# Order of loads, rope table per block, nine matmuls at the start: one change to a fused mLSTM and attention layer

## The chip, the cores and the metric

The kernel runs on one core of a Trainium2 chip. The metric is the device time of one execution in microseconds (us), lower is better. An engine takes its instructions in the order in which the program lists them for that engine: PE (TensorE, matrix products), ACT (ScalarE), DVE (VectorE), POOL (GpSimd), and SP (SyncE), which here issues nearly all the DMA transfers. An instruction that waits holds up everything behind it on its engine.

## The reference, cut to what matters

```python
SEQ, D_MODEL = 2048, 1024                 # one sequence, one layer
a   = rmsnorm(x, g_pre)
mix = concat(mlstm_4_heads(a), mla_8_heads(a)) @ w_out
x   = x + rmsnorm(mix, g_post)
m   = rmsnorm(x, g_pre_mlp)
x   = x + rmsnorm(relu(m @ w_up)**2 @ w_down, g_post_mlp)     # 1024 -> 4096 -> 1024

# mlstm: q, k = silu(conv4(a @ w)); v, output gate, input and forget gates from a;
#        chunk by chunk: num = (q k^T * D) v + w_inter * q C;   C = f' C + (i' k)^T v
# mla:   q from a latent of 256, k and v from a latent of 128, 32 rotated columns (rope),
#        softmax(q k^T / sqrt(96), causal) v
```

All data are float32.

## The kernel before, in words

Every large product is made in three matmul passes on a rounded part and a rest of each operand (`mm3`, L226 to L228): ACT rounds an operand (`wh`, `xh`, `ph`: "h" for high) and DVE or POOL subtracts to get the rest (`wl`, `xl`, `pl`). So each weight tile takes the path DMA load `wr`, ACT cast `wh` (L458), DVE or POOL rest `wl` (L463), then PE.

**Stages.** From 0 to about 540 us the input projection and the mLSTM run in four blocks of 512 tokens. A block works through units of 128 output columns: 13, 14, 15 (latents), 0 (gates), 1 to 4 (convolved q and k), 5 to 8 (mLSTM values, products `mv`), 9 to 12 (output gate), and the products of the latents `kp`, `vp`, `qp` and the rope part 17, 18. The mLSTM has four chunks of 128 tokens per block: chunk (b,c) loads its decay matrix `E` (L1157) and weights `iwbc` (L1165) from DRAM, ACT exponentiates `E` (L1172), PE forms `num` (L1192) and the state update `kv` (L1210), ACT squares `num` into `jk` (L1226), DVE writes `ho`, and a DMA stores it to `hT` (L1257). From about 540 to 980 us come the eight attention heads over four query blocks (scores `m` and `S`, probabilities `ph`/`pl`, output `o`), to about 1180 us the output projection, and then the MLP to the end.

**What sets the order.** `Plan.op` registers each piece of work with an engine, an estimated duration, a key (when it is wanted) and the tile buffers that it takes and frees. `Plan.run` plays the list through once and emits instructions in the order that results; `pin` (L236) fixes that order on PE, ACT, DVE and POOL. SP issues DMAs in the order of emission. A list of predecessors given to `pl.op` for a load moves only its place in that order; what is waited for at run time are the data and the buffers.

**Buffers near the change.** The results of `kp`, `vp`, `qp` and `rp` go through a ring of `SG = 4` staging tiles (`ks`, `vs`, `qs`, `rs`), each freed when its store to DRAM (`qkd`, `vd`, `qrd`) has ended. The attention's probabilities have `HB_`/`LB_` buffers of `ph` and `pl`. The rope table starts in block 0: DVE computes angles (`ang`, `kk`), ACT takes the sine, a store writes `trigd`, and `spread` (L1341) copies it row by row into the DRAM table `trep` for all 2048 positions; block b then loads its slice as `tb`. `rotate` (L869) rotates the one shared key row of a block.

**Hand-over to the attention.** While chunk (3,3) runs, SP also issues the first loads of the attention: `QK` (keys and queries of head 0, one group per block, L1499 and L1501), `maskneg`, and `V0` (L1511). The last values unit's evacuation `vext` (L1110) stands on ACT behind the exponentials of chunk (3,3), and the first score product `m` (L1537) needs the PSUM bank that it empties.

Of the kernel before, what the change touches and what calls it, by code (L numbers as in the profile page):

```python
# [10 lines left out]
F32 = mybir.dt.float32  # L11
# [7 lines left out]
P = 128  # L19
# [14 lines left out]
HB_ = 4  # L34
LB_ = 4
# [17 lines left out]
LEAD = 20.0  # L53
VLEAD = 6.0
# [3 lines left out]
BLOCK = 123.0  # L58
XLEAD = 20.0
WLEAD = 22.0  # L60
SPLIT = 10.0
XS0 = 12.0
XS1 = -60.0
CHUNK = 2.0
# [4 lines left out]
LGAIN = 20.0  # L69
CPOOL = True  # L70
KPOOL = ()
VPOS = (2, 2, 2, 4)
KROT = 50.0
# [10 lines left out]
WSTORE = 10.0  # L84
# [10 lines left out]
EV = 8.0  # L95
LASTLINE = [16, "k0", "k1", 9, "k2", "k3", "v0", 10, "v1", "v2", "v3", 11, 17, "q0", "q1", 12, "q2", "q3", 18, "r0", "r1", 5, 6, 7, 8]
LDK = 20.0
PQ = 0.0
# [24 lines left out]
class Plan:  # L123


    HOP, DMA, RATE, SUM = 190.0, 1900.0, 359.0, 4900.0
    late = 0.0

    def __init__(self):
        self.ops, self.rings, self.frees = [], {}, {}  # L130
        self.group, self.groups = None, {}
# [5 lines left out]
    def op(self, eng, ns, fn, after=(), key=0.0, take=(), free=(), kb=0):  # L137


        i = len(self.ops)  # L140
        self.ops.append((eng, ns, fn, list(after), key, take, kb))
        self.groups.setdefault(self.group, []).append(i)
        for ring, holder in free:
            self.frees.setdefault((ring, holder), []).append(i)
        return i

    def run(self):
# [24 lines left out]
        left, moved = len(ops), 0.0  # L172
        while left:
# [31 lines left out]
            end[i] = at[eng] = s + ops[i][1]  # L205
# [12 lines left out]
def trunk(ctx: ExitStack, tc: tile.TileContext, x, xT, pos, wu, wout, wup, wdn, cols, rows, consts, edge, out, dbg=None):  # L218
# [48 lines left out]
    trep = dram.tile([P, 2, SEQ], F32, tag="trep", name="trep")  # L267
# [70 lines left out]

    def load_cst():
        dma(cst[:, K_ID : K_ID + P], consts[:, K_ID : K_ID + P])  # L340
# [25 lines left out]
    def xsplit(b):  # L366
        def pair(j):
# [24 lines left out]
            for s in [slice(0, 1), slice(1, 2)] if b == 0 else [slice(0, 2)]:  # L392
                a = pl.op("SP", 500, lambda s=s: load(s), [first], key=kA(b, 0.65 * (2 * j + s.start) - 3 - XLEAD), kb=256 * (s.stop - s.start))
                for k in range(2 * j + s.start, 2 * j + s.stop):
                    at = kA(b, 0.65 * k - 3)
                    c = pl.op("Activation", 690, lambda k=k: hi(k), [a, o_col], at, take=(f"xh{k}",))
                    d = pl.op("DVE", 700, lambda k=k: lo(k), [c], at, take=(f"xl{k}",), free=[] if here else [("awr", first)])
# [44 lines left out]
    def wsplit(b, u):  # L442
# [27 lines left out]
        for s in pieces:  # L470
            n = s.stop - s.start
            a = pl.op("SP", 500, lambda s=s: load(s), [a0_], key=kA(b, at - WLEAD + WHALF * len(first)), kb=n / 2)
            c = pl.op("Activation", n * 0.833 + 110, lambda s=s: hi(s), [a], kA(b, at - SPLIT), take=() if first else ("wh",))
            d = pl.op(
                "Pool" if slow else "DVE", 148 + 2.104 * n if slow else n / 0.96 + 69, lambda s=s: lo(s), [c] + ([d] if first else []), kA(b, at - SPLIT), take=() if first else ("wl",),
# [127 lines left out]
    def latents_in(b):  # L603
# [4 lines left out]
        def one(i):  # L608
# [32 lines left out]
            if b == 0:  # L641
                o = pl.op("Activation", 560, evac, [u["op"], *t.get("o", [])], key, take=take, free=[("mm", u["head"])])
                head = o
                o = pl.op("DVE", 660, norm, [o, o_rsbc[b]], key, free=[("rsbc", o_rsbc[b])])
# [40 lines left out]
        def split(i):  # L685
# [8 lines left out]
            g = pl.op("DVE", 710, lambda: gain(i), [l, o], late, free=[("cbc", l)])  # L694
# [10 lines left out]
    def operands(b, t, o_c, held):  # L705
# [116 lines left out]
        o_tb = pl.op("SP", 500, table, [o_rope[2 * (b % 2) + 1], t["gained"]], kA(b, TIME[b][18] - 10), take=("cbc",), kb=512)  # L822
# [46 lines left out]
    def rotate(b, t, G):  # L869
# [26 lines left out]
        g = pl.op("SP", 500, load, [o_rope[2 * (b % 2)], G], key, take=("cth",), kb=128)  # L896
# [149 lines left out]
    def conv(b, j):  # L1046
# [39 lines left out]
        for i in range(1, 4):  # L1086
            o = pl.op("DVE", 720, lambda i=i: tap(i), [o], key, free=[("raw", r)])
# [3 lines left out]
            pl.op("DVE", 670, lambda i=i: put(i), [h, *war, *(o_fill3 if j < 2 else [])], key, free=[("cy", y), ("cth", h)])  # L1091
# [35 lines left out]
    def gates(b, h):  # L1127
# [11 lines left out]
        o_gate[b, h] = pl.op("DVE", 440, gain, [o], key)  # L1139

    def chunk(b, c):
# [119 lines left out]
        e = pl.op("SP", 500, load_e, [o_sc_in[b, "wd"]], key, take=("E",), kb=256)  # L1261
        i = pl.op("SP", 1000, load_w, [o_sc_in[b, "wd"]], key, take=("iwbc",), kb=128)
# [25 lines left out]
    def rope_tables():  # L1288
# [7 lines left out]
        def half(q):  # L1296
# [39 lines left out]
            def spread():  # L1336
                for hb in range(2):
                    cs = slice(hb * 1024 + q * 512, hb * 1024 + q * 512 + 512)
                    for x, r0, g0, n in ((0, 0, 0, 8), (1, 48, 0, 4), (1, 32, 4, 4)):
                        to = trep.rearrange("(g j) x t -> g j x t", j=16)[g0 : g0 + n, :, x, cs]  # L1340
                        dma(to, trigd[r0 : r0 + 16, cs].rearrange("(o j) t -> o j t", o=1).broadcast_to((n, 16, 512)))  # L1341

            r = pl.op("SP", 1000, load, [o_x[RB[q], RK[q]][1]], key, take=("raw",), kb=256)
            y = o = pl.op("DVE", 420, d0, [r], key, take=("cy",), free=[("raw", r)])
            o = pl.op("DVE", 480, d1, [o], key)
            h = o = pl.op("DVE", 480, d2, [o], key, take=("cth",))
            o = pl.op("DVE", 500, d3, [o], key)
            for c in (PI2_A, PI2_B, PI2_C):
                o = pl.op("DVE", 690, lambda c=c: d4(c), [o], key)
            o = pl.op("DVE", 480, d5, [o, o2], key)  # L1350
            o = pl.op("DVE", 430, d6, [o], key)
# [3 lines left out]
            o_rope.extend((o, pl.op("SP", 3000, spread, [o], key, kb=1024)))  # L1355
# [139 lines left out]
    def load_qk(h, b, key):  # L1495
# [8 lines left out]
        o = pl.op("SP", 1500, load, [*o_kd[h // 2, b], *o_qd[h // 2, b], o_qr[h // 4, b], o_s3 if s else o_s1, *war], key, kb=640)  # L1504
        o_q[h, b] = [o]
        o_k[h, b] = [o, o_kr[s, b]]

    def load_v(g, t, key):
# [4 lines left out]
        o_v[g, t] = [pl.op("SP", 1000, load, [o_vd[t], o_vd[t + 1], *([o_s3, o_const["v"]] if g else [o_s2, o_const["v0"]])], key, kb=512)]  # L1513
# [314 lines left out]
    def matrix(k):  # L1828
# [16 lines left out]
        a = pl.op("SP", 500, load, [o_s3 if early else o_left], key, take=("wr",), kb=512)  # L1845
        for c in range(2):
            b = pl.op("Activation", 610, lambda c=c: hi(c), [a], key, take=(ring[c],))
            o_w[k, c] = pl.op("DVE", 690, lambda c=c: lo(c), [b], key, free=[("wr", a)])
# [4 lines left out]
    def group(g):  # L1853
# [8 lines left out]
        def tile_(k):  # L1862
# [26 lines left out]
            if heads:  # L1889
                b = pl.op("SP", 1000, loadr, [o_left] + [o_out[h, blk][1] for h in heads], key, take=("rb",), kb=128)  # L1890
                r = pl.op("DVE", 335, norm, [a, b], key, free=[("rb", b)])
            c = pl.op("Activation", 307, hi, [r], key, take=(f"h{k}",))
            return c, pl.op("DVE", 335, lo, [c], key, free=[("hr", a)])
# [21 lines left out]
        def post(t):  # L1915
# [41 lines left out]
            f = pl.op("Pool" if slow else "DVE", 2300 if slow else 1140, add, [d, e], key, free=[("xt", d)])  # L1957
# [748 lines left out]
```

## Time and profile before

| | us |
|---|---|
| time, median of 3 runs | 2447.58 (2446.93 to 2453.14) |
| profiled execution, own time | 2449.75 |
| profiled execution, span in the trace | 2447.8 |
| PE busy in the span | 2384.2 (97%) |
| DVE busy | 1766.5 (72%) |
| ACT busy | 1360.5 (56%) |
| POOL busy | 835.1 (34%) |

Mean granted clock of PE: 0.993 of full speed. The views read below are the page with its chain of waits, the list of what PE waited for, tables of busy time by stretch of the span, and timelines. "Busy" counts an instruction from its modelled start to its modelled end. A row of the timeline gives start, duration, engine, line, operation, tiles, and in brackets the idle time before it with what ended it.

### The profile page before, as it was taken

The numbers are of one execution on the slowest core, as the hardware profiler recorded it, in microseconds if no ns is written. First come the engines' busy times: TensorE is split into PE (matmuls) and PEld (weight loads), VectorE is DVE, ScalarE is ACT, GpSimd is POOL, SyncE is SP. The second block draws the span as 40 slices with busy tenths as digits, with TensorE's granted clock in tenths as the row PEclk, the third lists the DMA queues.
The fourth block names the chain that finished last, engine by engine and source line by source line (L and its number), as shares of the span: only waits on it lengthen the run. The fifth ranks groups of instructions, "written<-read, shape, count | busy, mean of one in ns | idle before, by whom it ended". The sixth has DMA issues, their size and how long they took to land.

```text
span 2447.8 us, 34049 instructions
## 1 busy us (share of the span) xinstructions
PE 2384.2 (97%) x10915; PEld 1918.2 (78%) x10915; DVE 1766.5 (72%) x3153; ACT 1360.5 (56%) x2645; POOL 835.1 (34%) x713
## 2 busy tenths in 40 slices
PE   8899999999999999999999999999999999999998
PEld 6777787777777777788887888888888888888886
DVE  6766666648888888744866677766666687687889
ACT  5545444436777777644665666756665344343455
POOL 3433434436888788632100000000000232322346
PEclk9999999998999999999999999999999999999999
DMA  6696969797322220466777788756664534535348
GB/s 241 223 314 214 327 231 325 251 257 179 93 58 67 56 53 12 111 211 217 264 209 207 227 281 246 220 171 180 198 195 140 182 126 148 159 125 183 126 132 183
DMA packets 341819, 449.20 MB, mean 184 GB/s; under 512 B 34908, under 2 KB 227432, under 8 KB 341640
## 3 DMA queue, kind: packets, MB, share of 16 engines
q1 hardware_dynamic: 337704, 440.16, 58.2%
q0 software_dynamic: 3936, 6.87, 2.0%
q8 instruction: 86, 1.41, 0.2%
q14 instruction: 93, 0.76, 0.1%
HBM read 295.97 MB, written 153.05 MB: 183 GB/s over the span
## 4 chain that ended last, share of the span: by engine, by line
PE 78%; DVE 7%; DMA 6%; issue 3%; ACT 3%; POOL 2%; SPq 1%; DVEq 0%; ACTq 0%; POOLq 0%
PE mm L226 3%; PE mm L227 3%; PE mm L228 3%; PE S L226 3%; PE o L1622 2%; PE S L227 2%; PE S L228 2%; PE o L1625 2%; PE m L1537 2%; PE mv L227 1%; PE mv L228 1%; PE mv L226 1%; PE op L226 1%; PE op L228 1%; PE op L227 1%
## 5 line engine op out<-in xcount | busy, mean ns | idle before, releaser
L2516 POOL TENSOR_TENSOR y<-vd_0X,y 128x512 f32<-128x512 f32 x7 | 11.3, 1620 | 727.7 <-ACT vd_0X L2513 709.8
L1636 POOL TENSOR_TENSOR t<-t,ph 128x512 f32<-128x512 f32 (+1 forms) x192 | 214.4, 1116 | 17.8 <-ACT ph L1601 7.8
L1601 ACT ACTIVATE ph<-S 128x512 fp32r<-128x512 f32 (+1 forms) x320 | 170.2, 532 | 87.2 <-PE S L228 33.4
L2428 ACT CAST hh<-hr 128x512 fp32r<-128x512 f32 (+1 forms) x208 | 116.2, 567 | 150.5 <-DMA hr<-hd 23.8
L1609 DVE TENSOR_TENSOR pl<-S,ph 128x512 fp32r<-128x512 f32 (+3 forms) x272 | 156.7, 590 | 30.3 <-ACT S L1605 27.7
L226 PE MATMUL mm<-xh,wh 128*128 128x512 f32 x384 | 160.3, 417 | 17.1 <-ACT wh L458 8.4
L227 PE MATMUL mm<-xl,wh 128*128 128x512 f32 x384 | 151.7, 395 | 1.5 <-DVE xl L388 1.5
L228 PE MATMUL mm<-xh,wl 128*128 128x512 f32 x384 | 151.6, 395 | 0.7 <-DVE wl L463 0.7
L2433 DVE TENSOR_TENSOR hl<-hr,hh 128x512 fp32r<-128x512 f32 (+1 forms) x208 | 130.2, 637 | 28.2 <-ACT hh L2428 21.6
L1542 DVE TENSOR_REDUCE mp<-m 128x1 f32<-128x512 f32 x192 | 128.6, 681 | 27.1 <-PE m L1537 27.0
L1605 ACT ACTIVATE S<-S 128x512 f32<-128x512 f32 (+3 forms) x272 | 141.0, 519 | 0.3
L226 PE MATMUL S<-QK 97*128 97x512 f32 (+1 forms) x320 | 122.9, 384 | 6.2 <-DVE pl L1609 4.1
L1622 PE MATMUL o<-ph,V 128*128 128x512 f32 (+1 forms) x320 | 121.0, 378 | 0.2 <-DVE ot L1695 0.2
L1537 PE MATMUL m<-QK 96*128 96x512 f32 (+3 forms) x320 | 113.3, 399 | 6.8 <-ACT vext L1110 2.7
L227 PE MATMUL S<-QK 97*128 97x512 f32 (+1 forms) x320 | 118.3, 370 | 0.0
L228 PE MATMUL S<-QK 97*128 97x512 f32 (+1 forms) x320 | 117.9, 368 | 0.0
L1625 PE MATMUL o<-pl,V 128*65 128x512 f32 (+1 forms) x320 | 114.8, 361 | 0.2
L226 PEld LDWEIGHTS mm<-xh,wh 128*128 128x128 f32 x384 | 73.1, 190 | 38.3 <-ACT wh L458 8.4
L226 PE MATMUL op<-wo,hh 128*128 128x512 f32 x256 | 101.2, 395 | 0.7 <-DVE x L1937 0.7
L2267 ACT ACTIVATE t<-t 128x512 f32<-128x512 f32 x96 | 60.6, 631 | 73.8 <-DVE t L2262 73.2
L228 PE MATMUL op<-wo,hl 128*128 128x512 f32 x256 | 99.9, 390 | 0.0
L227 PE MATMUL op<-wo,hh 128*128 128x512 f32 x256 | 99.8, 390 | 0.0
(6442 smaller groups left out, 7581.2 us busy)
## 6 DMA issues: line engine op xcount, KB each, us to landing
hr<-hd SPq DMA_DIRECT2D x100, 448.0 KB
wr<-in_wu_dram SPq DMA_DIRECT2D x71, 512.0 KB
hd<-t SPq DMA_DIRECT2D x128, 256.0 KB
hd<-ts SPq DMA_DIRECT2D x96, 256.0 KB
wl<-wparts SPq DMA_DIRECT2D x45, 512.0 KB
QK<-qkd SPq DMA_DIRECT2D x32, 512.0 KB
xt<-in_x_dram SPq DMA_DIRECT2D x28, 512.0 KB
xf<-xd SPq DMA_DIRECT2D x40, 256.0 KB
```

Of the source, the lines that this page charges most:

```text
L226: pe.matmul(o, ah, bh, start=start, stop=False)
L227: pe.matmul(o, ah, bl, start=False, stop=False)
L228: pe.matmul(o, al, bh, start=False, stop=stop)
L1537: pe.matmul(ps[:, :n], Qh[s][0:96, q0 : q0 + P], Kh[s][0:96, kb * TB : kb * TB + n], start=True, stop=True)
L1542: vec.tensor_reduce(mp["t"][:, j, kb : kb + 1], ps, axis=AX.X, op=ALU.max)
L1601: act.activation(t["h"][:, :w], t["S"][:, :w], AF.Exp)
L1605: act.activation(t["p"][:, :w], t["S"][:, :w], AF.Exp)
L1609: (pool if by_pool else vec).tensor_tensor(t["l"][:, :w], t["p"][:, :w], f32(t["h"][:, :w]), ALU.subtract)
L1622: pe.matmul(o0, v[:, 0:128], t["h"][:, :w], start=start, stop=stop)
L1625: pe.matmul(o1, v[:, 64:129], t["l"][:, :w], start=start, stop=stop)
L1636: pool.tensor_tensor(to, to, hv, ALU.add)
L2433: vec.tensor_tensor(t["l", m][:, :w], t["r", m][:, :w], f32(t["h", m][:, :w]), ALU.subtract)
```

## The change

Constants first, since many edits are numbers of the planner:

```diff
-HB_ = 4 ; LB_ = 4 ; LEAD = 20.0 ; VLEAD = 6.0 ; BLOCK = 123.0
+HB_ = 5 ; LB_ = 5 ; LEAD = 25.0 ; VLEAD = 3.0 ; BLOCK = 119.0
+SPLIT0 = 30.0          # key lead of the weight splits in block 0 (SPLIT = 10 before)
+WARM = 9
-CHUNK = 2.0 ; LGAIN = 20.0 ; KPOOL = ()   ; KROT = 50.0 ; WSTORE = 10.0 ; EV = 8.0  ; PQ = 0.0
+CHUNK = 0.0 ; LGAIN = 40.0 ; KPOOL = (0,) ; KROT = 90.0 ; WSTORE = 5.0  ; EV = 15.0 ; PQ = 5.0
```

`LGAIN` is how late the latents' gain (`cca`, `ccb`) may come; `KPOOL = (0,)` puts the key rotation of block 0 (four operations of 32 x 512) on POOL instead of DVE. The planner also learns that a DVE operation with two inputs from SBUF ("DVES") takes longer while a long POOL operation runs; this changes order only. The other edits:

```diff
+    def warm():
+        act.copy(mrow[0:1, 16:17], zeros[0:1, 0:1])
+    def warm_pe():
+        ps = ps1.tile([P, 4, P], F32, tag="S", name="warm", bufs=2)
+        for i in range(WARM):
+            pe.matmul(ps[:, i % 4], ones, ones, start=True, stop=True)
...
-    trep = dram.tile([P, 2, SEQ], F32, tag="trep", name="trep")
+    trep = [dram.tile([P, 2, TB], F32, tag=f"trep{b}", name=f"trep{b}") for b in range(NB)]
...
-            dma(tb["t"], trep[:, :, bs])
+            dma(tb["t"], trep[b])
+        def spread():
+            for x, r0, g0, n in ((0, 0, 0, 8), (1, 48, 0, 4), (1, 32, 4, 4)):
+                to = trep[b].rearrange("(g j) x t -> g j x t", j=16)[g0 : g0 + n, :, x]
+                dma(to, trigd[r0 : r0 + 16, bs].rearrange("(o j) t -> o j t", o=1).broadcast_to((n, 16, TB)))
+        o = pl.op("SP", 1800, spread, [o_rope[b % 2], t["gained"]], kA(b, TIME[b][18] - 25), kb=512)
...
-            o_rope.extend((o, pl.op("SP", 3000, spread, [o], key, kb=1024)))
+            o_rope.append(o)
...
+    o_last = [o_chunk[NB - 1, 3]["e"], o_chunk[NB - 1, 3]["i"]]     # loads of E and iwbc of chunk (3,3)
-        o = pl.op("SP", 1500, load, [..., *war], key, kb=640)                                      # load_qk
+        o = pl.op("SP", 1500, load, [..., *war, *(o_last if b and not h else [])], key, kb=640)
...
+        if g: after = [o_s3, o_const["v"], o_sc[start_of[2, qb]]]                                  # load_v
+        else: after = [o_s2, o_const["v0"], *([o_sc[start_of[0, qb - 2]]] if qb > 1 else o_last if qb else [])]
...
-        a = pl.op("SP", 500, load, [o_s3 if early else o_left], key, take=("wr",), kb=512)         # output weights
+        a = pl.op("SP", 500, load, [o_sc[start_of[4, 0]] if early else o_left], key, take=("wr",), kb=512)
```

How this moves instructions, in the rows of the program order; a row has the source line, the operation, output and inputs (tile name, block and unit or chunk, buffer number) and the shape. The changed program's line numbers are some 32 to 40 higher.

On DVE, before, in block 0 behind the convolution of `raw0_1`: `ccb`/`cca` are the latents' gains, `qbd`/`cy`/`kT` the convolution, `wl0_5` to `wl0_8` the rests of the four values units.

```order
L681 SCALAR_TENSOR_TENSOR ccb0_325<-ccb0_325,col_61,cbc0_639 128x512
L1057 TENSOR_TENSOR raw0_2_688<-mm0_3_617,rsbc0_444 128x512
L681 SCALAR_TENSOR_TENSOR cca0_324<-cca0_324,col_61,cbc0_639 128x512 x2
L1078 SCALAR_TENSOR_TENSOR qbd0_111<-cth0_1_690,cy0_1_633 64x512 x2
L463 TENSOR_TENSOR wl0_5_733<-wr0_5_423,wh0_5_549 128x1024
L1069 SCALAR_TENSOR_TENSOR cy0_2_705<-raw0_2_688,col_61,cy0_2_705 128x512 x3
L463 TENSOR_TENSOR wl0_6_755<-wr0_6_451,wh0_6_621 128x1024
L1080 SCALAR_TENSOR_TENSOR kT0_113<-cth0_2_757,cy0_2_705 128x512
L463 TENSOR_TENSOR wl0_7_770<-wr0_7_452,wh0_7_673 128x1024
L463 TENSOR_TENSOR wl0_8_777<-wr0_8_501,wh0_8_735 128x1024
```

The same place of the changed program begins with the last of the four rests:

```order
L495 TENSOR_TENSOR wl0_8_748<-wr0_8_503,wh0_8_727 128x1024
L1109 SCALAR_TENSOR_TENSOR cy0_1_626<-raw0_1_245,col_61,cy0_1_626 128x512 x2
L1109 SCALAR_TENSOR_TENSOR cy0_2_742<-raw0_2_707,col_61,cy0_2_742 128x512
L1097 TENSOR_TENSOR raw0_3_772<-mm0_4_659,rsbc0_472 128x512
L1118 SCALAR_TENSOR_TENSOR qbd0_114<-cth0_1_774,cy0_1_626 64x512 x2
L1109 SCALAR_TENSOR_TENSOR cy0_2_742<-raw0_2_707,col_61,cy0_2_742 128x512 x2
L1109 SCALAR_TENSOR_TENSOR cy0_3_797<-raw0_3_772,col_61,cy0_3_797 128x512 x2
L1120 SCALAR_TENSOR_TENSOR kT0_116<-cth0_2_813,cy0_2_742 128x512
L1109 SCALAR_TENSOR_TENSOR cy0_3_797<-raw0_3_772,col_61,cy0_3_797 128x512
L714 SCALAR_TENSOR_TENSOR ccb0_337<-ccb0_337,col_61,cbc0_618 128x512
L714 SCALAR_TENSOR_TENSOR cca0_336<-cca0_336,col_61,cbc0_618 128x512 x2
```

`wl0_5` stands earlier still, ahead of the gate chain `sm0`; the gains have gone from ahead of the rests to behind the convolution. On PE, `num0_0` moved back by 27 matmuls, from among the first products of `mv0_2` to among the first of `mv0_3`.

On SP, before, in the second half of block 0 (`ks` are the staged keys, `xr1` the input of block 1):

```order
L763 DMA qkd_65<-ks0_0_1079 64x2x512 x2
L763 DMA qkd_65<-ks1_0_1083 64x2x512 x2
L453 DMA wr0_12_1161<-in_wu_dram 128x1024
L453 DMA wr0_18_1178<-in_wu_dram 128x512
L1341 DMA trep_69<-trigd_70 128x1x512
L1341 DMA trep_69<-trigd_70 64x1x512 x2
L1341 DMA trep_69<-trigd_70 128x1x512
L1341 DMA trep_69<-trigd_70 64x1x512 x2
L763 DMA qkd_65<-ks2_0_1176 64x2x512 x2
```

In the changed program, from the load of block 0's table to the same store:

```order
L853 DMA tb0_1125<-trep0_69 128x1024
L1374 DMA trigd_73<-kk1_972 64x512 x2
L570 DMA ddx1_1160<-rrx1_1153 4x128
L412 DMA xr1_0_1181<-in_xT_dram 128x2x512
L943 DMA krd_67<-tg0_1053 32x512
L796 DMA qkd_65<-ks2_0_1132 64x2x512 x2
```

Six table copies stood right ahead of the store of `ks2_0`. Now only three are issued in block 0 (`trep0`), ahead of the stores of `ks0_0` and `ks1_0` and of the last weight loads, and none stands between those and the store of `ks2_0`. The other nine follow in blocks 1 to 3, three each.

On SP at the hand-over, before:

```order
L1157 DMA E3_2_4810<-wd3_4289 128x512
L1499 DMA QK0_4769<-qkd_65 64x4x512
L1165 DMA iwbc3_2_4814<-wd3_4289 64x2x128 x2
L1501 DMA QK0_4769<-qrd_66 16x2x512 x2
L1499 DMA QK0_4769<-qkd_65 64x4x512
L1501 DMA QK0_4769<-qrd_66 16x2x512 x2
L1499 DMA QK0_4769<-qkd_65 64x4x512
L1501 DMA QK0_4769<-qrd_66 16x2x512 x2
L1499 DMA QK0_4769<-qkd_65 64x4x512
L1501 DMA QK0_4769<-qrd_66 16x2x512 x2
L1257 DMA hT_64<-ho3_0_4875 128x4x128
L1157 DMA E3_3_4896<-wd3_4289 128x512
```

And after the change:

```order
L1197 DMA E3_2_4828<-wd3_4296 128x512
L1471 DMA maskneg_4788<-in_consts_dram 128x512
L1526 DMA QK0_4787<-krd_67 32x2x512 x4
L1532 DMA QK0_4787<-qkd_65 64x4x512
L1205 DMA iwbc3_2_4834<-wd3_4296 64x2x128 x2
L1534 DMA QK0_4787<-qrd_66 16x2x512 x2
L1297 DMA hT_64<-ho3_0_4880 128x4x128
L1197 DMA E3_3_4887<-wd3_4296 128x512
L1205 DMA iwbc3_3_4910<-wd3_4296 64x2x128 x2
L1532 DMA QK0_4787<-qkd_65 64x4x512
L1534 DMA QK0_4787<-qrd_66 16x2x512 x2
```

The `QK` groups of blocks 1 to 3 and the `V0` loads went from ahead of `E3_3` to behind `E3_3` and `iwbc3_3`; `maskneg` and the rotated keys (`krd`), which stood ahead of `E3_2`, now stand behind it.

More of the change, by code (lines that the diff above doesn't have):

```diff
@@ L33 @@
 WHALF = 0.0
-HB_ = 4
-LB_ = 4
+HB_ = 5
+LB_ = 5
 TAIL = 2
@@ L52 @@
 TLATE = 0.0
[L53 to L54 removed]
+LEAD = 25.0
+VLEAD = 3.0
 SLEAD = 3.0
@@ L894, in lo @@
             eng.tensor_tensor(t["Gr"][s], t["G"][s], t["tg"][s], ALU.subtract)
-        g = pl.op("SP", 500, load, [o_rope[2 * (b % 2)], G], key, take=("cth",), kb=128)
+        g = pl.op("SP", 500, load, [o_rope[b % 2], G], key, take=("cth",), kb=128)
         o = pl.op(*cost, d1, [g, G], key)
@@ L1090, in conv @@
         o_qk[b, j] = [
-            pl.op("DVE", 670, lambda i=i: put(i), [h, *war, *(o_fill3 if j < 2 else [])], key, free=[("cy", y), ("cth", h)])
+            pl.op("DVES", 670, lambda i=i: put(i), [h, *war, *(o_fill3 if j < 2 else [])], key, free=[("cy", y), ("cth", h)])
             for i in range(2 if j < 2 else 1)
```

145 lines of the change are left out of this document (82 added, 63 removed).

## The prediction

> **What bounds the kernel now.** I read the page first, then PE by stretches, then the list of what PE waited for.
>
> ```profile
> PE 2384.2 (97%) x10915; PEld 1918.2 (78%) x10915; DVE 1766.5 (72%) x3153; ACT 1360.5 (56%) x2645; POOL 835.1 (34%) x713
> PE 78%; DVE 7%; DMA 6%; issue 3%; ACT 3%; POOL 2%; SPq 1%; DVEq 0%; ACTq 0%; POOLq 0%
> ```
>
> PE is busy for all but 2447.8 - 2384.2 = 63.6 us, and the matmuls stay the same, apart from nine added ones. So the change can win only PE's idle time and the time that PE runs at a lower clock. The next table has the stretch in us, its length, busy time of PE, PEld, DVE, ACT, POOL (instructions in brackets), granted clock, DMA share, GB/s.
>
> ```profile
> 0.00:123.00 123.00, 106.21 (x474) 84.33 (x474) 85.51 (x173) 66.26 (x124) 50.15 (x51) 0.97 0.69 232
> 123.00:246.00 123.00, 114.85 (x528) 92.29 (x529) 79.45 (x155) 57.50 (x110) 46.25 (x41) 0.99 0.78 263
> 246.00:369.00 123.00, 120.94 (x567) 96.96 (x566) 79.32 (x169) 61.21 (x124) 46.08 (x43) 1.00 0.80 280
> 369.00:492.00 123.00, 116.83 (x529) 90.84 (x528) 79.54 (x158) 55.80 (x104) 53.71 (x46) 1.00 0.85 288
> 492.00:615.00 123.00, 116.25 (x538) 90.57 (x537) 80.40 (x197) 60.72 (x144) 63.51 (x64) 0.92 0.83 215
> 2300.00:2448.00 148.00, 137.23 (x599) 111.55 (x597) 130.37 (x187) 76.82 (x178) 74.98 (x70) 0.98 0.65 155
> ```
>
> Idle per stretch: 16.8, 8.2, 2.1, 6.2, 6.8, and 10.8 in the tail. That is 40 us to 615 us and only 13 us in the 1,685 us after it up to the tail. The clock is below 1 at the beginning and around the hand-over. What PE waited for (total, times, longest):
>
> ```profile
> PE mm L226 <- ACT wh L458: 8.4, 1, 8.4
> PE mv L227 <- DVE wl L463: 4.9, 2, 3.3
> PE mm L226 <- ACT vs L784: 4.3, 1, 4.3
> PE S L226 <- DVE pl L1609: 4.1, 9, 1.3
> PE m L1537 <- ACT vext L1110: 2.7, 1, 2.7
> ```
>
> The waits on `wl`, `vs` and `vext` are three places, and each is followed by a stretch at half the clock:
>
> ```profile
> 8.30:12.70 4.40, 4.33 (x10) 3.42 (x11) 4.28 (x7) 4.35 (x8) 0.00 (x0) 1.00 1.05 393
> 59.70:63.90 4.20, 0.92 (x5) 0.76 (x5) 4.17 (x3) 1.84 (x5) 3.76 (x3) 1.00 0.03 12
> 64.00:70.70 6.70, 5.12 (x12) 3.50 (x12) 6.59 (x9) 1.80 (x5) 2.79 (x3) 0.50 0.89 265
> 124.20:128.60 4.40, 0.08 (x2) 0.07 (x1) 2.08 (x3) 1.17 (x3) 0.41 (x2) 1.00 0.91 334
> 128.80:132.20 3.40, 3.40 (x9) 2.61 (x9) 2.94 (x4) 2.86 (x5) 1.64 (x2) 0.50 0.73 166
> 538.60:541.70 3.10, 0.39 (x3) 0.30 (x2) 0.91 (x2) 2.62 (x12) 2.21 (x4) 1.00 0.92 270
> 541.90:548.60 6.70, 6.03 (x21) 5.25 (x21) 4.64 (x16) 0.00 (x0) 0.93 (x1) 0.50 1.17 294
> 548.70:555.40 6.70, 4.99 (x21) 2.43 (x19) 6.38 (x23) 2.55 (x11) 1.01 (x1) 1.00 0.78 207
> 555.50:569.10 13.60, 13.14 (x39) 9.59 (x40) 8.27 (x20) 4.54 (x11) 3.10 (x7) 0.50 0.94 221
> ```
>
> Nine matmuls take 3.40 us at clock 0.50. At half clock the busy time counts double, so half of it is lost. The first stretch (8.30) shows 1.00 but only 10 matmuls in 4.40 us, which is the same slow pace. These places are where the change acts.
>
> **The change part by part.** All sums are made against the profiled execution's own 2449.75 us, which is 2.2 above the median of the runs shown (2447.58).
>
> *Start.*
>
> ```profile
> 0.94 0.17 DVE L331 MEMSET ones<- 128x128 f32 x1
> 2.19 5.49 DMA wr<-in_wu_dram
> 7.70 1.24 ACT L458 CAST wh<-wr 128x512 fp32r<-128x512 f32 x2 [0.59 <-DMA wr<-in_wu_dram]
> 29.76 0.89 PE rp L590 x8
> ```
>
> The first real matmul waits for the cast of a weight tile that lands at 7.7 us. Loading ACT's table earlier moves the `xh` casts but not this one, so its gain is 0. The four 128 x 128 products of `rp` (eight rows) took 0.89 us, 0.22 each, or 0.44 at half clock. Nine of them on `ones`, ready at 1.1 us, run until about 1.2 + 4.0 = 5.2 us, beside the load. Then PE is idle for some 3.1 us until 8.37. Warmth that lasts would save half of the slow stretch, (12.7 - 8.37)/2 = 2.2 us. In this trace idle times of 2.7 us (before 541.4) and 3.3 us (before 63.0) were each followed by half clock. I take 0, with bounds 0 and -2.2.
>
> [...]
>
> *Block 0, the rests of the values weights (59.7 to 70.7).*
>
> ```profile
> 48.35 1.37 DVE L1078 SCALAR_TENSOR_TENSOR qbd<-cth,cy 64x512 f32<-64x512 f32 x2
> 57.27 3.48 DVE L1078 SCALAR_TENSOR_TENSOR qbd<-cth,cy 64x512 f32<-64x512 f32 x2
> 60.78 2.18 DVE L463 TENSOR_TENSOR wl<-wr,wh 128x1024 fp32r<-128x1024 f32 x1
> 65.49 1.22 DVE L463 TENSOR_TENSOR wl<-wr,wh 128x1024 fp32r<-128x1024 f32 x1
> ```
>
> DVE reaches `wl0_5` only at 60.8, behind the gains and `qbd`, and both are stretched: 3.48 against 1.37 us and 2.18 against 1.22 us, while POOL is busy 3.76 of 4.20 us (the row of 59.70). PE loses 3.3 + 1.6 = 4.9 us waiting, and 5.12/2 = 2.6 us by the clock, together 7.5. In the changed order all four rests stand ahead of most of the convolution, and the gains behind it. That removes both waits. What is late next is the gate chain `sm0`, behind which `wl0_5` no longer waits, and with it `E0_0`. `num0_0` stands 27 matmuls later on PE (27 x 0.24 = 6.5 us, by the step of one matmul in the chain, quoted in the next part), about as much as the four rests put ahead cost at 1.22 to 2.18 us each (4.9 to 8.7). So up to 2.5 us of new wait is possible. I take -6, with bounds 0 and -7.5.
>
> *Block 0, the staging ring (100 to 132).*
>
> ```profile
> 112.45 4.51 SPq L1341 DMA_DIRECT2D trep<-trigd  x6
> 117.26 1.27 SPq L763 DMA_DIRECT2D qkd<-ks  x2
> 117.92 9.13 DMA qkd<-ks
> 127.17 0.70 DVE vs L787
> 106.51 0.24 PE mm L226
> PE mm L226 <- ACT ks L733: 1.8, 2, 1.3
> ```
>
> Six table copies (0.75 us of SP each, 1 MB together) stand right ahead of the store of `ks2_0`. That store takes 9.13 us, and the staging tile that `vs` needs is free only then. PE stood 4.3 us, and 1.8 in smaller waits at the same ring just ahead (the last row, of the waits from 90 to 140 us); the clock costs 3.40/2 = 1.7 more. Total 7.8. Now only three copies are issued in block 0, ahead of the stores, and none between. SP is free 4.5 us sooner for `ks2_0`, and the transfer has less beside it, but the weights and inputs of block 1 stay (DMA share 0.91). The wait of 4.3 needs 4.3 us: 4.5 at SP alone cover it, if the smaller waits stay. I take -6, which is the 4.3 and the 1.7 behind it, with bounds 0 and -7.8.
>
> *Tables of later blocks.* Blocks 1 to 3 get three copies each: 2.25 us of SP and 0.5 MB, some 1.9 us of transfer at 263 to 288 GB/s. Block loads are wanted well ahead, so they hide behind queued tiles; without this cover each block would pay up to 2.25. I take +1 in all (0 to +2, one block in the open).
>
> *Hand-over (538 to 569).*
>
> ```profile
> 523.60 0.69 DVE L1253 TENSOR_TENSOR ho<-ht,gate 128x512 f32<-128x512 f32 x1 [0.59 <-PE ht L1249]
> 530.47 0.53 SPq L1257 DMA_DIRECT2D hT<-ho  x1
> 531.09 0.45 SPq L1157 DMA_DIRECT2D E<-wd  x1
> 538.00 1.28 ACT L1172 ACTIVATE E<-E,tm 128x128 f32<-128x128 f32 x4 [9.44 <-DMA E<-wd]
> ```
>
> `ho` of chunk (3,0) was done at 524.3, but its store went out only at 530.5, behind the `QK` groups on SP, and `E3_3` behind it. ACT waited 9.44 us for that `E`, with `jk` and `vext` queued behind. So `m` started 2.7 us late, with 0.7 more idle in the next stretch (6.70 - 6.03) and 6.03/2 = 3.0 by the clock: 6.5 together. Now `hT` and `E3_3` stand ahead of the later `QK` groups. `E3_3` can go out near 525 instead of 531.1; six us are more than the 2.7 that PE waited, and the wait goes. What is late next: the `QK` and `V0` loads of later blocks, behind it; block 0's `QK`, which the first scores read, stays ahead. The second slow stretch (13.14/2 = 6.6) follows 6.7 us in which DVE was busy 6.38 with the first maxima and PE 4.99. The changed order doesn't remove that work. I take half, -3.3. Sum -9.8, bounds 0 and -13.1.
>
> *Edits with no price of their own.* The key rotation on POOL: four operations of 32 x 512, with POOL idle 72.9 of the first 123 us and the result first read by `QK` at the hand-over; 0, and its cost without cover is bounded by the stretch in the rows of 57 to 61 us, some 3 us on DVE. Later V and output weight loads fall where PE is the bound and are read much later: 0; if one were late, 0.5 MB at 215 GB/s is 2.4 us. A fifth `ph`/`pl` buffer: at most the 4.1 us of waits for `pl`; I take -1. The tail: DVE is busy 130.37 of 148 us there and the same operations stay, so 0 (-3 to +4, from the 10.8 us idle and as a third of it either way). The changed keys shift the other waits of blocks 1 to 3, 8.2 + 2.1 + 6.2 - 4.3 = 12.2 us idle; I take -1.5 (-5 to +5).
>
> **Sum:** 0 - 6 - 6 + 1 - 9.8 - 1 - 1.5 = -23.3, or 2449.75 - 23.3 = 2426.4 against the profiled execution and 2447.58 - 23.3 = 2424.3 against the median. I predict **2425**.
>
> **The rivals.**
>
> *The waits move and do not go.* `num0_0` waits for `E0_0` in place of `mv` for `wl`, the staging ring waits for the same store behind the loads of block 1, or `m` waits for DVE. For it: DVE is 70% busy in block 0 and the DMA queues 0.91 at the staging wait, neither of which gets less. Against it: each wait has a named instruction ahead that moves. It gives a net gain of about 3: 2445.
>
> *All clear.* The full bounds at the three places, -7.5 - 7.8 - 13.1, the warm start's -2.2 and -4 around them give -34.6: 2413. For it: the slow clock comes as a consequence of waits; against it: DVE's reductions after the hand-over.
>
> *The warm clock holds at the start.* Inside my forecast: 2449.75 - 25.5 = 2424.2, against the median 2422. One in four, since 2.7 us of idle were enough for half clock here.
>
> *Slower: DVE becomes the bound of block 0.* The rests, convolution and gains between 40 and 123 us all have to pass DVE beside POOL. If DVE's operations were stretched there throughout by the 3.48/1.37 or 2.18/1.22 of the rows, 85.51 x 83/123 = 58 us of DVE work would become more than the 83 us available; the point from which it decides is 83/58 = 1.4. At 1.7 it is 98 us, 15 too many, in place of the 12 gained there, with the half clock after it (2 or 3): +17, and with the other terms as taken (1 - 9.8 - 1 - 1.5 = -11.3) +6, with the hand-over's gain at nothing +15: 2453 to 2463. Against it: POOL is busy only 50.15 of 123 us, and only one more small job goes there.
>
> *It does not do what it says.* The waits for the DMA data remain whatever the order: that is the first rival's price.
>
> **How the numbers follow.** Forecast, 2416 to 2440: 0.66. All clear, below 2416: 0.11. Waits move, 2440 to 2453: 0.16. Slower: 0.07. The range goes to 2410, below the sum of all bounds, and to 2446, just over the first rival's time; it leaves some 0.05 below and 0.15 above (half of that rival, and all of the slower one). What a measurement of this kernel can tell from no change is about 0.3%, 7.3 us: faster than 2440.3 is 0.66 + 0.11 = 0.77, within is 0.16, slower is 0.07.
>
> **What would show it.** In the changed profile: no wait of `mv` for `wl` of over 1 us and clock 1.00 around 60 to 70 us; no wait for `vs` or `ks` of over 2 us around 100 to 130 us; `E` of chunk (3,3) issued before 527 us, and no wait for `vext`; the second slow stretch in the first scores halved. PE's idle time up to 615 us should fall from 40 to about 25. Wrong would be: a new wait of `num` for `E` near 80 us, the ring waiting again behind block 1's loads, new idle in blocks 1 to 3, or clock 0.50 after the hand-over as before.

## The result, and the profile after

| | before | after |
|---|---|---|
| median, us (5 runs each, beside each other) | 2449.17 (2446.93 to 2453.14) | 2428.12 (2425.68 to 2430.62) |
| profiled execution, own time | 2449.75 | 2430.62 |
| span in the trace | 2447.8 | 2428.9 |

The ratio is 0.9913 with a 95% interval of 0.9899 to 0.9926: 21 us faster, where 2425 was predicted. The profiled execution is the slowest of the five, and it is the one whose trace is read here. First its page, then busy time by the same stretches as before (the last one ends with the span):

```profile
PE 2376.6 (98%) x10933; PEld 1920.0 (79%) x10933; DVE 1748.1 (72%) x3149; ACT 1362.3 (56%) x2646; POOL 832.7 (34%) x717
```

```profile
0.00:123.00 123.00, 112.81 (x509) 90.33 (x510) 94.04 (x174) 72.21 (x133) 59.13 (x59) 1.00 0.72 242
123.00:246.00 123.00, 120.28 (x567) 97.03 (x566) 82.05 (x171) 57.20 (x118) 52.32 (x46) 1.00 0.78 267
492.00:615.00 123.00, 118.88 (x589) 93.83 (x588) 90.42 (x226) 68.02 (x164) 71.69 (x73) 0.94 0.84 193
2300.00:2428.00 128.00, 111.92 (x479) 91.26 (x477) 100.11 (x153) 65.98 (x159) 64.65 (x64) 0.94 0.68 150
```

In the first 123 us PE starts 509 matmuls where it started 474, and the idle time fell from 16.8 to 10.2 us. Part of this is the nine added matmuls, which the trace shows as 18 instructions; they are all that PE does in the first 7.3 us:

```profile
0.00:7.30 7.30, 4.21 (x18) 3.91 (x18) 1.87 (x8) 3.03 (x5) 1.18 (x9) 1.00 0.66 182
```

So 491 of the 509 are the kernel's own, and 4.2 of the 6.6 us of idle time that went are filled with work that nobody needs. Around the hand-over the clock is still at 0.94 in the mean, and in the tail it fell from 0.98 to 0.94 with 16 us idle out of 128: the tail has become worse. The list of waits has no `wl` of 3 us, no `vs` of 1 us (the longest is 0.8) and no `vext` any more; at its head stands a wait of the tail:

```profile
PE d_7X L2519 <- DVE y L2542: 3.0, 1, 3.0
...
PE mm L245 <- DVE ks L769: 2.1, 2, 1.8
...
PE mt L1609 <- DVE mp L1583: 1.9, 1, 1.9
```

Where the time went is read best from groups of matmuls by tile: each row ends with the starts of its first and last instruction. Of before, and then of after:

```profile
L226 PE MATMUL qp<-ch,wh x32: 394/397/400, 135.7 to 500.3; 128*128 128x512 f32 x32
L1622 PE MATMUL o<-ph,V x320: 220/393/628, 564.9 to 1026.2; 128*128 128x512 f32 x144, 128*128 128x256 f32 x16
L2478 PE MATMUL d_0X<-d,hh x64: 388/389/392, 1818.1 to 2373.9; 128*128 128x512 f32 x64
L2480 PE MATMUL d_7X<-d,hl x64: 387/390/498, 1888.6 to 2438.0; 128*128 128x512 f32 x64
```

```profile
L245 PE MATMUL qp<-ch,wh x32: 392/397/422, 125.4 to 487.1; 128*128 128x512 f32 x32
L1663 PE MATMUL o<-ph,V x320: 221/393/628, 545.4 to 1001.3; 128*128 128x512 f32 x144, 128*128 128x256 f32 x16
L2519 PE MATMUL d_0X<-d,hh x64: 389/389/392, 1791.5 to 2346.4; 128*128 128x512 f32 x64
L2521 PE MATMUL d_7X<-d,hl x64: 388/389/628, 1862.3 to 2414.6; 128*128 128x512 f32 x64
```

The differences between these rows give the account of the 18.9 us of span, stage by stage:

| stretch, by its last mark | mark before, after | won so far | won in the stretch | predicted for it |
|---|---|---|---|---|
| input projection and mLSTM (last `qp`) | 500.3, 487.1 | 13.2 | 13.2 | 12.5 |
| hand-over (first `o`) | 564.9, 545.4 | 19.5 | 6.3 | 9.8 |
| attention (last `o`) | 1026.2, 1001.3 | 24.9 | 5.4 | 1 |
| output projection, up (first `d_0X`) | 1818.1, 1791.5 | 26.6 | 1.7 | 0 |
| down and tail (end of the span) | 2447.8, 2428.9 | 18.9 | -7.7 | 0 |

The sum came out near because errors of opposite signs offset each other: the attention won 4.4 us more than predicted, while the hand-over won 3.5 less and the tail gave back 7.7. The 1.7 us of the output projection and the up projection are smaller than their scatter: this stretch takes 790.2 us here, and 788.5, 787.7 and 788.3 us in three of the kernels below whose edits lie outside it (no matmuls at the start, the old tail, the first filling). The experiments ask for the causes.

### The profile page after: what moved, and what is told of

Its sections match the earlier page's. It is cut to its first block, busy times and chain, and to the rows that moved or that the text cites. A ratio compares the mean times of both kernels' runs of the same rounds, so it can differ in the third digit from the quotient of the medians.

```text
span 2428.9 us, 33978 instructions
## 1 busy us (share of the span) xinstructions
PE 2376.6 (98%) x10933; PEld 1920.0 (79%) x10933; DVE 1748.1 (72%) x3149; ACT 1362.3 (56%) x2646; POOL 832.7 (34%) x717
## 4 chain that ended last, share of the span: by engine, by line
PE 53%; DVE 1%; DMA 1%; ACT 0%; issue 0%; DVEq 0%; SPq 0%; POOL 0%; ACTq 0%; POOLq 0%
PE op L245 1%; PE op L247 1%; PE op L246 1%; DMA hr<-hd 1%; PE d_1X L2519 1%; PE d_1X L2520 1%; PE d_3X L2520 1%; PE d_3X L2519 1%; PE d_2X L2519 1%; PE d_2X L2520 1%; PE d_1X L2521 1%; PE d_2X L2521 1%; PE d_7X L2519 1%; PE d_3X L2521 1%; PE d_6X L2519 1%; PE d_0X L2520 1%
```

## The experiments

Each kernel is the changed one with one edit, unless said otherwise. Times are medians; the ratio to before, measured beside it on the same chip, is the safer number across the groups of runs, since before itself read 2446 to 2449 in them. The changed kernel's ratio is 0.9913.

**The order of loads at the hand-over undone.**

```diff
-        o = pl.op("SP", 1500, load, [..., *war, *(o_last if b and not h else [])], key, kb=640)
+        o = pl.op("SP", 1500, load, [..., *war], key, kb=640)
-            after = [o_s2, o_const["v0"], *([o_sc[start_of[0, qb - 2]]] if qb > 1 else o_last if qb else [])]
+            after = [o_s2, o_const["v0"], *([o_sc[start_of[0, qb - 2]]] if qb > 1 else [])]
```

> The changed kernel with one part undone: the QK loads of blocks 1 to 3 and the V0 loads again go out ahead of E and iwbc of chunk (3,3) (only SP's order differs). Theory: the 7 us that the changed kernel gained between the last values products and the first attention output come back, E of chunk (3,3) is issued about 6 us later than in the changed kernel, ACT waits for it with vext or jk behind, and the time is 2432 to 2436. Rival: the gain there came from the order of DVE and ACT at the hand-over, not from the load; then the time is within 2 us of the changed kernel's 2428.

Measured: 2431.35 us, ratio 0.9930 (0.9918 to 0.9942). The timelines of ACT, SP and PE around the load of `E` for chunk (3,3), of the changed kernel and then of this one:

```profile
511.88 0.33 SPq L1197 DMA_DIRECT2D E<-wd  x1
516.76 1.28 ACT L1212 ACTIVATE E<-E,tm 128x128 f32<-128x128 f32 x4 [0.55 <-DMA E<-wd]
```

```profile
515.50 0.45 SPq L1197 DMA_DIRECT2D E<-wd  x1
522.52 1.28 ACT L1212 ACTIVATE E<-E,tm 128x128 f32<-128x128 f32 x4 [7.66 <-DMA E<-wd]
525.16 0.68 ACT L1150 ACTIVATE vext<-mv,rsx 128x512 f32<-128x512 f32 x1
525.89 0.56 PE L1578 MATMUL m<-QK 96*128 96x256 f32 x2 [0.93 <-ACT vext L1150]
```

`E` is issued 3.6 us later, ACT waits 7.66 instead of 0.55 us with `vext` behind, and PE waits for it again. From the last `qp` to the first `o` this kernel takes 62.4 us (485.7 to 548.1), the changed one 58.3. So the mechanism is as predicted, and the order of loads alone is worth 3 to 4 us: 3.2 by the medians and 4.2 by the ratios, whose intervals overlap, 4.1 by the stretch itself. A time of 2432 to 2436 was expected. What won the rest of the 6.3 us there was not tried.

**The rests of block 0 late again.**

```diff
-SPLIT0 = 30.0 ; LGAIN = 40.0
+SPLIT0 = 10.0 ; LGAIN = 20.0
```

> The changed kernel with the old lead of the weight splits in block 0 and the old lead of the latents' gains (SPLIT0 = 10, LGAIN = 20). Theory: wl0_5 comes late on DVE again, PE waits 3 to 5 us for it near 60 us and the clock drops to 0.50 behind it, +5 to +7.5 us: 2433 to 2436. Rival: the planner's stretched DVE durations alone keep the rests early, and the time stays within 2 us of 2428.

Measured: 2431.92 us, ratio 0.9935 (0.9921 to 0.9948). In the list of waits from 40 to 123 us:

```profile
PE mv L246 <- DVE wl L495: 4.7, 1, 4.7
```

The wait for `wl` is back, and the first `qp` starts at 131.0 instead of 125.4 us. At the last `o` the whole 5.8 us are still there (1007.1 against 1001.3), at the first `d_0X` 3.2 (1794.7 against 1791.5). Whether the rest was made up is not shown: the stretch between these marks takes 787.6 us here, no less than in the three kernels named under the table. The edit costs 3.8 us by the medians, a little under what was expected, and 5.4 by the ratios.

**The table in two halves again.** The edit restores `trep` as one DRAM tile, six copies per half.

> The changed kernel with one part undone: the rope table again is one DRAM tensor of all positions, copied in two halves of six DMAs in block 0. Theory: the second half of the copies stands ahead of the stores of the staged keys again, PE waits for the staging ring near 100 to 130 us, +3 to +8 us: 2431 to 2436. Rival: the earlier order of block 0 alone already keeps the stores clear of the copies; then 2426 to 2430.

Measured: 2433.52 us, ratio 0.9941 (0.9928 to 0.9953). The time came back, but not where it was expected. The waits from 90 to 145 us:

```profile
PE qp L245 <- DVE gate L1170: 2.6, 1, 2.6
PE mm L245 <- DVE ks L769: 1.7, 1, 1.7
PE ptx L562 <- POOL rsx L558: 1.6, 1, 1.6
PE vp L245 <- ACT ks L766: 1.0, 1, 1.0
PE vp L245 <- DVE vs L820: 0.7, 1, 0.7
```

PE does not stand 4 us for the staging ring. Its waits there (`ks`, `vs`) come to 3.4 us, where the changed kernel has 2.1 in the same window; the longest wait is for the output gate, and one is for the row statistics `rsx`, both on other engines. The edit also moved instructions on DVE in these blocks, so that this run does not separate the copies' bandwidth from the order that follows from them. At the last `qp` 3.4 us are lost (490.5 against 487.1). A single wait of 4.8 us of `o` near 575 us adds to the profiled execution, which is the slowest of the six.

**Four buffers for the probabilities again.**

```diff
-HB_ = 5 ; LB_ = 5
+HB_ = 4 ; LB_ = 4
```

> The changed kernel with four instead of five buffers for ph and pl. Theory: between the first attention output and the output projection PE loses the 3 to 4 us that the changed kernel gained there (many small waits of S for pl and of o for ph), 2431 to 2433. Rival: that gain comes from other parts of the order, and the time stays within 1.5 us of 2428.

Measured: 2435.25 us, ratio 0.9951 (0.9938 to 0.9964). It has the highest median of the parts undone by themselves, about 7 us above the changed kernel (9 by the ratios), where 3 to 5 were expected. The loss lies in the attention: from the first to the last `o` this kernel takes 464.2 us (543.9 to 1008.1), the changed one 455.9. The waits from 555 to 1000 us, of the changed kernel and then of this one:

```profile
PE o L1663 <- DVE ot L1736: 2.1, 5, 0.7
PE S L245 <- DVE pl L1650: 1.9, 4, 0.8
```

```profile
PE o L1666 <- POOL pl L1650: 2.0, 2, 1.7
PE S L245 <- DVE pl L1650: 1.5, 3, 0.9
PE S L245 <- ACT p L1646: 1.5, 2, 0.8
PE m L1578 <- DVE mp L1583: 1.3, 4, 0.3
```

The waits of `S` for `pl` are about the same; grown or new are waits for `p`, for the row maxima `mp` and for POOL's `pl`. This fits a fifth buffer that lets ACT, DVE and POOL all run ahead, and not only the one wait that names `pl`. But these waits do not explain the size: PE's idle time between the two marks grew by 2.8 of the 8.3 us. Why PE also counts as busy for 5.5 us longer, with 2308 matmuls against 2301 and the clock at 1.00 in both, stays open.

**No matmuls at the start, and nearly twice as many.**

```diff
-WARM = 9
+WARM = 0     # and, in the other kernel, WARM = 17
```

> The changed kernel without the nine matmuls on ones; ACT's early copy stays. Theory: the nine matmuls gave nothing, since the clock was at half again until about 12 to 14 us with them: 2426 to 2430, the same as the changed kernel. Rival: they gave up to 2 us: 2430 to 2432.

> The changed kernel with 17 matmuls on the tile of ones instead of 9, so that PE has work from 1.2 us to about the first weight tile at 7.9 us. [...] Rival: the clock at the start depends on something other than PE's gap (time since the start, or the size of the matmuls); then the real matmuls stay at half clock until about 13 us and the time is 2428 or up to 1 us more.

Measured: 2427.93 us without (0.9918, 0.9904 to 0.9931), 2424.53 with 17 (0.9905, 0.9891 to 0.9918). Busy time from 7.8 to 13.6 us, of the changed kernel and of the one with 17 on ones, and from that kernel's waits up to 60 us the longest behind the start:

```profile
7.80:13.60 5.80, 5.75 (x14) 4.44 (x15) 5.09 (x8) 4.77 (x8) 0.00 (x0) 1.00 1.03 376
```

```profile
7.80:13.60 5.80, 5.44 (x24) 3.56 (x23) 4.87 (x8) 4.60 (x7) 0.00 (x0) 1.00 1.03 373
```

```profile
PE rp L623 <- POOL rsx L558: 1.4, 1, 1.4
```

Nine matmuls change nothing in the time, as predicted, and the changed kernel gets 14 real matmuls into this stretch. With 17 most run 0.23 us apart from 8.1 us on, where it was 0.43 until 13.6 us; ten of them at the shorter step would save 2 us, an estimate from these two steps. The row counts 24, of which three belong to the last of the 17 and 21 are real. But the seven matmuls gained are lost again by 33 us: the first matmul of `rp`, which waits for statistics of the input, starts at 32.9 us against 32.4. That the time is 3.6 us lower is within what the intervals leave open; the profiled execution is the slowest of the four, the others lie at 2424 to 2425.

**The planner's stretched durations taken away everywhere.**

```diff
-    BESIDE, HEAVY = 0.75, 1100.0
+    BESIDE, HEAVY = 0.0, 1100.0
```

> The changed kernel with the planner's stretching of DVE operations beside POOL taken away everywhere (BESIDE = 0); every other edit stays. The order of all engines changes with it. Theory: the tail gives back its 8 to 9 us, the places that the hand-made edits cover (the rests in block 0, the table, the hand-over, the buffers) stay won, and block 0 to the hand-over loses at most 4 by waits that the stretching had foreseen: 2419 to 2424. Rival: the stretching is what won most of the time before the tail; then 2430 or more.

Measured: 2443.78 us, ratio 0.9983 (0.9975 to 0.9992). The theory fell and the rival on record holds: nearly all of the gain is gone, although every hand-made edit is in. The slowness that these durations model shows in the trace of before: two `qbd` operations take 3.48 us beside POOL (busy for all 3.60 us from 57.2 us on) and 1.37 us with little of it (0.57 of the 1.50 us from 48.3 us on). The waits from 40 to 123 us:

```profile
PE mv L245 <- DVE raw L1097: 5.1, 1, 5.1
PE S L1193 <- DVE kT L1120: 4.2, 1, 4.2
```

With the rests ahead and an order made for an unhindered DVE, the convolution comes late, and PE waits for it instead: the first `qp` starts at 137.9 us, 2.2 later than in the kernel before. The loss grows through blocks 1 to 3, to 22.2 us at the last `qp` (509.3 against 487.1), and hardly grows behind it. From the last `qp` to the first `o` it takes 59.0 us (58.3 in the changed kernel), the attention takes the same 455.9, and the part from the first `d_0X` on is 7.2 us shorter, as with the old tail below. So the gain that hangs on the stretched durations lies in the order of the projection and the mLSTM.

This looks like the slower rival of the prediction, DVE as the bound of block 0, but it is not the same. The busy time from 40 to 123 us, of the changed kernel and then of this one:

```profile
40.00:123.00 83.00, 76.84 (x357) 60.49 (x357) 73.74 (x147) 48.78 (x98) 45.91 (x42) 1.00 0.63 203
40.00:123.00 83.00, 70.11 (x307) 55.24 (x307) 63.04 (x135) 41.20 (x89) 38.42 (x37) 0.92 0.52 168
```

DVE is busy 63 of the 83 us here and 74 in the changed kernel. It does not run out of time; it does its work in an order in which PE waits.

**The tail.** Two kernels give the operations of the last stage their old durations: only the final scaling (L2615 and its neighbours), or these and the rests `hl` of the last operands.

```diff
-                b = pl.op("DVES", 750, lambda e=e: both(e), [o, o_dw], key, free=[("fsm", sq[0])])
+                b = pl.op("DVE", 750, lambda e=e: both(e), [o, o_dw], key, free=[("fsm", sq[0])])
...
-            d = pl.op("DVES", 66 + 1.22 * nj * P, lambda m=m: lo(m), ...)     # in the second kernel alone
+            d = pl.op("DVE", 66 + 1.22 * nj * P, lambda m=m: lo(m), ...)
```

> The changed kernel with the old durations for the final scaling operations alone; the rests of the last operands keep the stretched ones. Theory: the scaling operations that stand between y's evacuations on DVE are what PE's d_7X waits for; moving them back alone removes the 3 us wait and most of the tail's loss: 2419 to 2423. Rival: the order of the rests (hl) decides; then 2425 or more.

> The changed kernel with the planner's stretching taken away for the operations of the last stage alone (final scaling and the rests of the last operands), which brings DVE's order in the last 40 us near that of before; nothing else moves. Theory: the 3 us wait of d_7X for y, the half clock behind it and the longer end of the chain (together about 7 to 8 us against before) go: 2420 to 2424. Rival: the tail is lost because the last operand load hr lands late and whatever the order, DVE is the bound there; then 2426 to 2430.

Measured: 2421.16 us with the scaling alone (0.9890, 0.9876 to 0.9903), 2418.94 with both (0.9882, 0.9867 to 0.9897). What they remove stands in the timeline of the changed kernel:

```profile
2399.60 1.40 DVE L2615 SCALAR_TENSOR_TENSOR y<-y,fsm,gpm 128x512 f32<-128x512 f32 x2
2400.92 0.68 DVE L2542 TENSOR_TENSOR y<-d_6X,y 128x512 f32<-128x512 f32 x1
2401.52 1.41 DVE L2615 SCALAR_TENSOR_TENSOR y<-y,fsm,gpm 128x512 f32<-128x512 f32 x2
2402.84 0.69 DVE L2542 TENSOR_TENSOR y<-d_7X,y 128x512 f32<-128x512 f32 x1
2403.67 0.77 PE L2519 MATMUL d_7X<-d,hh 128*128 128x512 f32 x1 [3.01 <-DVE y L2542]
```

and in its table by stretches:

```profile
2399.60:2402.90 3.30, 1.06 (x5) 0.55 (x3) 3.30 (x7) 1.98 (x7) 2.79 (x4) 1.00 1.04 124
2403.00:2409.80 6.80, 6.13 (x15) 4.81 (x16) 3.11 (x6) 0.74 (x3) 4.49 (x5) 0.50 1.08 168
```

Four scaling operations (2.8 us) stand between the additions that empty PE's banks. PE waits 3 us and then runs 6.8 us at half clock, and the scaling still left comes after the last matmul: 2428.9 - 2414.6 = 14.3 us of span remain there, 9.8 before. With both edits PE waits at most 0.6 us at this place, and 9.8 us remain after the last matmul (2416.0 - 2406.2).

**Filling the wait at the hand-over.** PE waits 1.85 us for `mt`'s bank at 532 us, and about 13 us at half clock follow. Two kernels put matmuls that nobody needs there: seven into the same bank, in the changed kernel; eight into a free bank of another pool, with the old tail.

```diff
+            if (h, qb) == (0, 0):
+                spare = ps1.tile([P, 4, P], F32, tag="S", name="spare", bufs=2)
+                for i in range(8):
+                    pe.matmul(spare[:, i % 4], f32(identr), f32(identr), start=True, stop=True)
             t["p"] = bank(len(reds), f"mt{h}_{qb}")
```

> The changed kernel with seven 128 x 128 matmuls that compute nothing needed (they write into the PSUM tile of mt before mt itself does) put on PE ahead of the first mt, where PE waits 1.85 us for the first maxima. Theory: the half clock from 536 to 549 us follows a stretch of about 3.4 us in which PE was busy for only half; filled, that stretch is busy for 0.9 or more, the clock stays at 1.00, and some 6 to 7 us go: 2421 to 2423. Rival: the clock drops for another reason (the kind of work, DVE's load); then the stretch at 0.50 stays and the time is 2427 to 2430.

> The changed kernel with the old durations in the last stage (as in tail_order_old) and eight 128 x 128 matmuls that compute nothing needed, ahead of the first mt, this time into a free PSUM tile of another pool, so that they run in PE's 1.85 us wait there and not behind it. Theory: the stretch of 3.4 us with PE busy for half is filled, the clock stays at 1.00 behind it at least until the next gap, and 1 to 5 us go against tail_order_old's 2419: 2414 to 2418. Rival: DVE is the bound in these 15 us, a faster PE only waits for it, the clock drops one stretch later and nothing is won: 2418 to 2421.

Measured: 2427.59 us (0.9923, 0.9910 to 0.9936) for the first. Its matmuls waited for the same bank, so they ran behind the wait and filled nothing; the run tells nothing of the theory. The second took 2419.23 us (0.9882, 0.9869 to 0.9896), the same as `tail_order_old`, whose stretches come first here, then its own:

```profile
530.60:534.00 3.40, 1.53 (x10) 1.13 (x11) 3.21 (x14) 1.08 (x3) 1.01 (x1) 1.00 1.19 290
534.00:537.40 3.40, 3.00 (x8) 1.82 (x7) 3.34 (x11) 0.00 (x0) 0.00 (x0) 0.50 1.02 268
...
563.30:570.00 6.70, 6.05 (x30) 4.74 (x30) 6.11 (x14) 4.53 (x10) 6.27 (x7) 1.00 0.17 30
```

```profile
530.60:534.00 3.40, 3.21 (x24) 2.69 (x25) 3.19 (x12) 0.85 (x3) 1.01 (x1) 1.00 1.18 291
534.00:537.40 3.40, 2.51 (x11) 1.49 (x11) 3.39 (x10) 0.24 (x2) 0.00 (x0) 1.00 1.02 268
...
563.30:570.00 6.70, 5.21 (x14) 3.88 (x15) 4.66 (x10) 3.34 (x8) 3.28 (x3) 0.50 0.18 38
```

And from that kernel's waits between 525 and 580 us:

```profile
PE o L1667 <- DVE ot L1740: 3.0, 1, 3.0
```

The filling holds the clock at 1.00 through the hand-over, and the first `o` starts 2.9 us earlier (540.8 against 543.7). Then `o` waits 3.0 us for `ot`, where the other kernel waits 0.65, the clock drops there, and all is given back: the attention ends later (last `o` at 1001.2 against 999.6). The rival was right in its main point: in these 40 us a faster PE only comes to wait for DVE. The medians alone would leave a gain of a few us open.

**Three edits together:** 17 matmuls, the old tail, the seven matmuls into `mt`'s bank.

> Three edits together on the changed kernel: 17 matmuls on ones, the old durations for the operations of the last stage, and the seven filling matmuls at the hand-over. Theory: the tail's -9 and the hand-over's -6 to -7 add, and the start gives 0 to -2 (its earlier clock is met by a wait for rsx near 33 us): 2410 to 2414. Rival: the filling gives nothing and only the tail counts: 2417 to 2420.

Measured: 2425.88 us, ratio 0.9914 (0.9902 to 0.9927), worse than the old tail alone. In its trace the seven matmuls only delay the hand-over (first `o` at 546.6 against 543.7), and a wait of 1.85 us of the output projection near 1118 us adds. The time is far from the 2410 to 2414 expected. Which of these is chance was not tried again.

**The best version** is the changed kernel with the old durations in the tail: 2418.94 us, about 9 us below the changed kernel and 29 below before.

**Not tried alone** were the other constants of the change (`LEAD`, `VLEAD`, `BLOCK`, `CHUNK`, `KPOOL`, `KROT`, `WSTORE`, `EV`, `PQ`) and the later loads of the output weights. The costs of the four parts undone above need not add, and what these constants are worth stays open.

## Why the prediction was right, and where it was off

*Start, taken as 0.* Right: no matmuls and nine give the same time. The rival of a lasting warm clock is out for nine: behind 2.5 us of idle the real matmuls are 0.43 us apart until 13.6 us. When 17 do hold it (0.23 us apart), the next wait takes the gain in the profiled execution, which the prediction did not consider.

*Block 0, the rests and the ring, -6 and -6, and blocks 1 to 3.* Right in sum: 13.2 won up to the last `qp` against 12.5. Putting the rests back brought a wait of 4.7 us and 5.6 us by the first `qp`, near the -6. The reason given for the ring, SP's free 4.5 us, is not shown: with the table in halves most of the time went to other waits. The sign that was named, PE's idle time up to 615 us falling from 40 to about 25, came true with 25.6, but only because the added matmuls count as 4.2 us of work; without them it is 29.8.

*Hand-over, -9.8.* The mechanism was right and the size too large. The half of the second slow stretch, -3.3, is the term that failed: the clock was still at half for about 13.6 us (535.9 to 549.5), as long as before (555.5 to 569.1), and the filled kernel shows that a faster PE there only waits for DVE a little later. So this time at half clock was no loss to be won back. Without it the term is -6.5, against 6.3 measured; that these lie so near is in part luck, since the order of loads, the reason given, is shown for only 3 to 4 of them.

*A fifth buffer, taken as -1, at most -4.1.* Too small: the attention won 5.4 us, and undoing the buffers alone costs about 7 (2435.25 against 2428.12). The bound was wrong in kind: it counted only the waits of `S` for `pl`, while waits for `p`, `mp` and POOL's `pl` came with the fourth buffer too. Even all of these are smaller than the loss, so the mechanism is known only in part.

*The tail, taken as 0 (-3 to +4).* This step failed: +7.7. The prediction argued that DVE has the same operations in both, and took the order to be worth at most a third of 10.8 us idle. What decides is which of DVE's operations PE waits for, and four that PE does not wait for went ahead of one that it needs. The program fixes DVE's order ahead of the run, so this could have been read from the last 15 us of that order.

*The slower rival.* The price was real and the mechanism another: with the same edits but an order that takes DVE for unhindered, PE waits for DVE in block 0 and the gain shrinks to 4 us, though DVE is busy only 63 of 83 us there, where the rival needs more than 83. In the changed kernel DVE is busy for 74 of them, 9 more than before, and PE waits less.

The forecast thus held by its largest place, block 0, and in the mechanism at the hand-over. That it came within 3 us of the measured median is luck: errors of 3.5 to 8 us with opposite signs lie behind it.

## What to carry to other kernels

Where a list scheduler sets the order, the model of durations is part of the change: the same edits were worth 21 us with DVE's slowness beside POOL (`qbd`: 3.48 against 1.37 us) in the model and 4 without it, and the same model, applied to the tail, cost 9. When an in-order engine serves a waiting one, put what the other waits for ahead of what nobody waits for, above all near the end. Before paying for a stretch at half clock, ask whether the engine is the bound there.

## What the runs showed of the hardware

PE's clock fell behind stretches in which PE was busy for a third to three quarters of the time. The clock column reads 1.00 at the head of a span even over slow matmuls, as from 8.30 to 12.70 us in the kernel before (ten matmuls in 4.40 us) and up to 13.6 us in the changed kernel (10 in the 3.30 us from 10.3, 16 in the 3.30 us from 13.7), so the 1.00 of the first row below says nothing. In the kernel with the late rests the nine matmuls at the start fell so that a stretch of 3.40 us was nearly full (3.27 us busy, where the changed kernel has 2.24 of its first 3.40 us and 1.87 of the 3.30 us from 3.5). There the column falls to 0.50 by 9.0 us and is back at 1.00 by 12.4:

```profile
2.10:5.50 3.40, 3.27 (x16) 2.97 (x14) 0.24 (x1) 0.91 (x2) 0.00 (x0) 1.00 0.82 235
5.60:8.90 3.30, 1.16 (x4) 0.68 (x5) 2.26 (x4) 2.30 (x4) 0.00 (x0) 1.00 0.98 324
9.00:12.30 3.30, 3.30 (x9) 2.48 (x9) 3.02 (x5) 2.65 (x5) 0.00 (x0) 0.50 1.00 357
12.40:15.70 3.30, 3.30 (x15) 2.46 (x14) 2.18 (x3) 2.23 (x4) 1.53 (x2) 1.00 1.03 417
```

The clock was lost here behind a stretch with PE busy for 1.16 of 3.30 us, in the tail behind 1.06 of 3.30, and at the hand-over behind 1.53 of 3.40 (with the old tail). In the kernel before it was lost at 555.45 us behind a stretch that counts as busy for 2.63 of 3.41:

```profile
552.04:555.45 3.41, 2.63 (x9) 1.23 (x9) 3.41 (x11) 0.00 (x0) 1.01 (x1) 1.00 0.38 93
```

In the changed kernel one that counts as busy for 1.65 of 3.41 us (92.16 to 95.57) kept it. So in these runs the share of busy time alone does not tell whether the clock falls. Nor did one full stretch bring the clock back at the hand-over: with the old tail PE is busy for all 3.40 us of the stretches from 537.4, 540.8 and 544.2 us, and the clock stays at 0.50 until 547.6.
